# Operand places and dummy products in the three-part matrix products, and the last attention head's statistics turned by copies within SBUF

## The chip, the cores and the metric

The kernel runs on one core of a Trainium2 chip. The metric is the device time of one execution in microseconds (us). Three executions of the kernel before took 1504.59, 1506.12 and 1506.7 us; their median is 1506.12 us.

## What is computed

Two transformer layers on 512 tokens of width 1024, in fp32. Layer 0 mixes tokens with a gated linear recurrence, layer 1 with dilated attention in three groups of 8 heads; each is followed by a gated feed-forward network. Cut to what the change touches:

```python
def dilated_attention_mixer(u, cos, sin, w_in, w_out):
    proj = (u @ w_in).reshape(B, S, N_GROUPS, 3, ATT_HEADS, ATT_HEAD_DIM)   # 3 groups: (128,1) (512,4) (2048,16)
    for gi, (window, dilation) in enumerate(DILATED_GROUPS):
        q = apply_partial_rope(proj[:, :, gi, 0], cos, sin) * scale
        k = apply_partial_rope(proj[:, :, gi, 1], cos, sin)
        o_g, lse_g = dilated_group_attention(q, k, proj[:, :, gi, 2], window, dilation)
    wts = jax.nn.softmax(jnp.stack(lses, axis=0), axis=0)
    o = jnp.einsum('gbsh,gbshd->bshd', wts, jnp.stack(outs, axis=0))
    return o.reshape(B, S, D_MODEL) @ w_out

def swiglu_ffn(u, w_in, w_out):                     # D_FF = 2816 = 22 x 128
    gate, up = jnp.split(u @ w_in, 2, axis=-1)
    return (jax.nn.silu(gate) * up) @ w_out
```

## The kernel before, in words

**Three products for one.** Each operand is split into a high part (ACT, a cast to fp32r) and a low part (DVE, the difference). One product of 128x128 blocks becomes three fp32r matmuls: high by high, high by low, low by high (`three`, L576 to L579, and the loops at L964 and L1982). Each matmul has a stationary operand (128 columns, loaded by LDWEIGHTS) and a moving operand that streams past it.

**Seven for eight.** Most of the feed-forward input products (`seven_products`, L882), the queries and keys of groups 1 and 2 (`sevens`) and the values of groups 1 and 2 (`value_unit`) go by a scheme of seven half-size block products. They are *narrow*: the moving operand has 256 columns. One of the seven is a *unit*: 4 blocks of 128 rows, each by three matmuls, so 12 matmuls in a row into one PSUM place (a value product is two units, for two blocks of 128 tokens). The other products have a moving operand of 512 columns.

**The feed-forward stretches.** `seven_products` works through 16 functions (128 columns of gate and up) in layer 0 and 18 in layer 1. Per function `run` (L960) issues seven units: `first` with `B11`, `both` with `T3`, and so on. For function 0 `B11` is the first 256 tokens of `uh`, `ul` where they lie; then `shift()` (L893) copies them 144 columns further, and the functions after it take the copy.

**The attention as a plan.** Units, casts, softmax steps and DMAs of layer 1's attention are recorded as tasks with a cost and a due time (`Plan`); `Plan.run` tries 72 rules on a model of the engines and issues the best order, and each engine then runs its queue strictly in that order. `ticks` gives each head's steps their place: scores of group 0, of 1, of 2 (`scores_of`), the merge of the softmax statistics over groups (`merged`), transposes of the probabilities (`flipped`, PR for groups 1 and 2 by residue, PN for group 0), sums with the values (`sums_r`, `sums_n`). The 8 heads' output is multiplied by the output weights (`out_prods`, three matmuls of 512 columns, called a *group* below). The last head's late steps lie among the groups of the first columns of that product: after the products of each kt the table at L2446 says how many ticks to take.

**The turn of the statistics.** Group 0 has maximum and sum per token in natural order, groups 1 and 2 in residue order (token = 4 l + r). Both orders are needed in both places, so `scores_of` writes them to memory and reads them back in the other order: four DMAs on POOL's queue, L2261 (write of group 0's), L2281 (read back, "oR"), L2287 (write of the others'), L2289 (read back, "oN"). `merged` waits for both reads.

**Places.** By the addresses in the built program, the two operands of a narrow matmul start, modulo 256 bytes, here (all others of a kind alike, since blocks and tiles are multiples of 256 bytes apart):

| narrow matmuls | count | moving | stationary | stationary less moving |
|---|---|---|---|---|
| feed-forward, all but the next row (L964) | 2472 | 128 | 192 | 64 |
| feed-forward, `first` with the shifted `B11` (L964) | 384 | 192 | 192 | 0 |
| the first functions of a feed-forward and the like (L577 to L579, L825, L828) | 384 | 128 | 192 | 64 |
| queries and keys (L1982) | 1344 | 128 | 192 | 64 |
| values (L1982): the weights move, the tokens stand | 672 | 0 | 128 | 128 |

`R0` and `V0` (L37) are the columns by which the split tiles are set off: 16 fp32 (64 bytes) where weights are stationary, 32 (128 bytes) where value weights move.

Of the kernel before, what the change touches and what calls it, by code (L numbers as in the profile page):

```python
# [11 lines left out]
F32 = mybir.dt.float32  # L12
# [5 lines left out]
P = 128  # L18
# [3 lines left out]
NT = S // P  # L22
DFF = 2816
NF = DFF // P
NH = 8
# [11 lines left out]
R0, V0 = 16, 32  # L37
# [103 lines left out]
class Plan:  # L141
# [5 lines left out]
    def __init__(self):  # L147
        self.tasks, self.names, self.seq = [], {}, {}
# [144 lines left out]
def block_kernel(tc, x, c, positions, ada_w, ada_b, norm_g, hgrn_w_in, lower, hgrn_norm_g, hgrn_w_out,  # L293
                 attn_w_in, attn_w_out, ffn_w_in, ffn_w_out, inv_freq, out):
    nc = tc.nc
# [6 lines left out]
    with ExitStack() as ctx:  # L302
# [579 lines left out]
        def seven_products(fs, mid, seeded, spare, th, tl):  # L882
# [8 lines left out]
            B11 = [u_of(0, 0), [(uh[:, k, 144:400], ul[:, k, 144:400]) for k in range(4)]]  # L891

            def shift():  # L893

                for a, b in ((112, 256), (0, 112)):
                    for copy, t in ((act.copy, uh), (dve.tensor_copy, ul)):
                        copy(t[:, 0:4, a + 144:b + 144], t[:, 0:4, a:b].bitcast(F32))
# [77 lines left out]
            with tc.manual_schedule(engines=ORDERED):  # L975
# [10 lines left out]
                for i in range(len(fs)):  # L986
# [3 lines left out]
                    run(s.first, R, 0, B11[i > 0], True)  # L990
# [13 lines left out]
                    if i == 0:  # L1004
                        shift()
# [970 lines left out]
        def products(cost, dst, key, terms, begin, reads):  # L1976


            def go():
                todo = [p for t in terms() for p in t]  # L1980
                for i, (x, y) in enumerate(todo):
                    pe.matmul(dst(), x, y, start=begin and i == 0, stop=i == len(todo) - 1, skip_group_check=True)  # L1982
            of_units.append(len(plan.tasks))
            PE(cost, go, reads, [key])

# [119 lines left out]
        def plain(g, hd):  # L2105
# [16 lines left out]
            def both():  # L2122
# [4 lines left out]
                def one(i, t):  # L2127
                    b = mm_of()
                    for part in range(4):
# [4 lines left out]
                        products(6 * 0.2275, lambda: b.t, b(), terms, part == 0, [p("h", i), p("l", i)])  # L2134
# [15 lines left out]
        def value_unit(i, hf):  # L2150
# [46 lines left out]
            def run(tag, tile, o, us):  # L2197
                b, p = mm_of(tag), ps[tile]
                for n in range(2):
# [4 lines left out]
                    products(12 * 0.1165, lambda n=n: b.t[:, n * 256:(n + 1) * 256], b(), terms, n == 0, [p("h", o), p("l", o)])  # L2204
# [28 lines left out]

        def scores_of(hd, g):
# [3 lines left out]
            if g == 0:  # L2238
# [42 lines left out]
            POOL(0.6, lambda: pool.dma_start(so.t[:, 1, 0], scr[hd, 0].rearrange("(l r) s -> l r s", r=4)), [("scr", hd, 0)], [so("oR")], late=4.5)  # L2281
            DVE(0.12, lambda: dve.tensor_tensor(so.t[:, 0, 0, :, 0], mR.t[:, 0], mR.t[:, 1], op=OP.max), [mR(i, r) for i in (1, 2) for r in range(NT)], [so("R")])
            DVE(0.12, lambda: dve.tensor_scalar(nR.t, so.t[:, 0, 0, :, 0], -1.0, None, op0=OP.mult), [so("R")], [nR()])
            for r in range(NT):
                ACT(0.52, lambda r=r: act.activation(PR[:, r], PR[:, r], AF.Exp, bias=nR.t[:, r:r + 1], accum_out=so.t[:, 0, 0, r, 1:2]),
                    [nR(), so("R")], [("PR", 0, 1, r), ("PR", 0, 2, r), so("R", r)])
            POOL(0.6, lambda: pool.dma_start(scr[hd, 1].rearrange("(l r) s -> l r s", r=4), so.t[:, 0, 0]), [so("R")] + [so("R", r) for r in range(NT)],  # L2287
# [3 lines left out]
        def merged(hd):  # L2291
# [4 lines left out]
            reads = [so("R"), so("oR"), so("oN")] + [so(n, t) for n in "RN" for t in range(NT)]  # L2296
# [142 lines left out]
        for kt in range(KT):  # L2439
# [6 lines left out]
            for _ in range({0: 4, 1: 1, 2: 1, 3: 1, 5: 1, 6: 1}.get(kt, 0)):  # L2446
                ticks.tick()
# [53 lines left out]
```

## Time and profile before

| | us |
|---|---|
| median of 3 runs | 1506.12 |
| the profiled execution's own time | 1504.35 |
| its span, first to last instruction | 1502.6 |
| PE busy (matmul) | 1476.8 |
| DVE busy | 1095.8 |
| ACT busy | 797.2 |

The span is 1.75 us shorter than the execution; times of single instructions count from the span's start. PE is the engine of the matmuls (its weight loads are PEld), DVE, ACT and POOL are the vector, scalar and GpSimd engines, SP issues most DMAs. A matmul's duration in the profile (0.28 us for 256 columns) is its way through the array and overlaps its neighbours; what a stream costs is the distance from one start to the next, called the *pitch* here.

### The profile page before, as it was taken

How to read it: one execution, taken by the hardware profiler on the slowest of the kernel's cores; microseconds unless marked ns; L12 is line 12 of the kernel's file. 1: busy time of each engine (PE TensorE's matmuls, PEld its weight loads, DVE VectorE, ACT ScalarE, POOL GpSimd, SP SyncE). 2: the span in 40 equal slices, each digit the busy share in tenths (PEclk: the TensorE clock that was granted, in tenths of full speed). 3: DMA queues.
4: the chain of work that ended last, by engine and by line, in shares of the span. 5: the costliest groups of instructions: out<-in, count | busy, mean ns of one | idle time of the engine just before them, and what ended most of it. 6: DMA issues, size and time to landing. Idle time of an engine off the chain costs nothing. (4 is left out here: it accounts for less than half of the span.)

```text
span 1502.6 us, 25061 instructions
## 1 busy us (share of the span) xinstructions
PE 1476.8 (98%) x9823; PEld 1323.5 (88%) x9823; DVE 1095.8 (73%) x1800; ACT 797.2 (53%) x1474; POOL 191.3 (13%) x172
## 2 busy tenths in 40 slices
PE   8999999999999999999999999999989999999998
PEld 6777788888999988788999999999978899999886
DVE  4587678487688885777798877888666978887533
ACT  4433343373455542267647878477875555555231
POOL 1011011031111100131001010001012211110100
PEclk9999999999999999999999999999999999999999
DMA  9654555124233346634344442345243333333531
GB/s 308 183 170 140 183 169 169 57 79 146 85 113 113 113 161 211 220 117 143 113 120 144 109 136 73 118 131 147 89 134 119 104 94 113 113 113 141 197 111 56
DMA packets 210151, 201.09 MB, mean 134 GB/s; under 512 B 8248, under 2 KB 167920, under 8 KB 209776
## 3 DMA queue, kind: packets, MB, share of 16 engines
q1 hardware_dynamic: 207056, 192.71, 41.3%
q10 hardware_dynamic: 1952, 6.65, 1.2%
q8 instruction: 77, 1.26, 0.4%
q0 software_dynamic: 1024, 0.13, 0.2%
q14 instruction: 42, 0.34, 0.1%
HBM read 192.31 MB, written 5.31 MB: 132 GB/s over the span
## 5 line engine op out<-in xcount | busy, mean ns | idle before, releaser
L90 ACT CAST hi<-raw 128x2048 fp32r<-128x2048 f32 x43 | 82.1, 1909 | 144.3 <-DMA raw<-in_ffn_w_out_dram 74.9
L91 DVE TENSOR_TENSOR lo<-raw,hi 128x2048 fp32r<-128x2048 f32 x43 | 103.7, 2413 | 65.7 <-ACT hi L90 65.6
L577 PE MATMUL ps_mm<-uh,hi 128*128 128x512 f32 (+1 forms) x400 | 145.6, 364 | 0.0
L578 PE MATMUL ps_mm<-ul,hi 128*128 128x512 f32 (+1 forms) x400 | 144.5, 361 | 1.1 <-DVE ul L677 1.1
L579 PE MATMUL ps_mm<-uh,lo 128*128 128x512 f32 (+1 forms) x400 | 143.9, 360 | 0.0
L1982 PE MATMUL ps_mm<-apart,hiq 128*128 128x256 f32 (+1 forms) x608 | 142.0, 326 | 0.1
L1982 PEld LDWEIGHTS ps_mm<-apart,hiq 128*128 128x128 f32 x608 | 100.0, 189 | 8.4 <-ACT xs L2096 0.3
L1982 PE MATMUL ps_mm<-apart,loq 128*128 128x256 f32 (+1 forms) x304 | 97.4, 321 | 0.4 <-DVE loq L2118 0.4
L964 PE MATMUL ps_mm<-tl,hiq 128*128 128x256 f32 x340 | 94.0, 276 | 0.0
L964 PE MATMUL ps_mm<-th,hiq 128*128 128x256 f32 x340 | 94.0, 276 | 0.0
L964 PE MATMUL ps_mm<-th,loq 128*128 128x256 f32 x340 | 94.0, 276 | 0.0
L955 DVE TENSOR_TENSOR loq<-raw,hiq 128x1024 fp32r<-128x1024 f32 x68 | 80.3, 1221 | 18.6 <-ACT hiq L951 18.6
L577 PEld LDWEIGHTS ps_mm<-uh,hi 128*128 128x128 f32 x400 | 75.2, 188 | 18.2 <-issue 6.7
L578 PEld LDWEIGHTS ps_mm<-ul,hi 128*128 128x128 f32 x400 | 75.4, 189 | 12.3 <-DVE ul L677 1.5
L579 PEld LDWEIGHTS ps_mm<-uh,lo 128*128 128x128 f32 x400 | 75.1, 188 | 12.4 <-issue 1.1
L578 PE MATMUL ps_mm<-lo,oh 128*128 128x512 f32 x208 | 81.5, 392 | 2.4 <-DVE lo L91 2.4
L935 POOL TENSOR_TENSOR raw<-raw 128x512 f32<-128x512 f32 x34 | 44.8, 1318 | 303.1 <-DVE spare L931 138.5
L577 PE MATMUL ps_mm<-hi,oh 128*128 128x512 f32 x208 | 81.5, 392 | 0.0
L951 ACT CAST hiq<-raw 128x1024 fp32r<-128x1024 f32 x68 | 68.0, 1047 | 18.7 <-DVE raw L939 17.1
L1982 PE MATMUL ps_mm<-uh,hiq 128*128 128x256 f32 x256 | 71.9, 281 | 0.0
L1982 PE MATMUL ps_mm<-uh,loq 128*128 128x256 f32 x256 | 71.3, 279 | 0.0
L1982 PE MATMUL ps_mm<-ul,hiq 128*128 128x256 f32 x256 | 71.3, 278 | 0.0
(479 smaller groups left out, 4632.8 us busy)
## 6 DMA issues: line engine op xcount, KB each, us to landing
raw<-in_ada_w_dram SPq DMA_DIRECT2D x40, 1024.0 KB, 5.1
raw<-in_ffn_w_in_dram SPq DMA_DIRECT2D x136, 256.0 KB, 4.1
raw<-in_ffn_w_out_dram SPq DMA_DIRECT2D x22, 1024.0 KB, 5.1
raw<-in_attn_w_in_dram SPq DMA_DIRECT2D x64, 256.0 KB, 4.6
raw<-in_hgrn_w_in_dram SPq DMA_DIRECT2D x12, 1024.0 KB, 5.3
raw<-in_attn_w_in_dram SPq DMA_DIRECT2D x12, 1024.0 KB, 5.2
raw<-in_ffn_w_in_dram SPq DMA_DIRECT2D x10, 1024.0 KB, 6.5
raw<-in_attn_w_in_dram SPq DMA_DIRECT2D x16, 512.0 KB, 4.6
```

The source lines that it names most:

```text
L90: self.nc.scalar.copy(hi, t)
L91: self.nc.vector.tensor_sub(lo, t, hi.bitcast(F32))
L577: pe.matmul(ps, ah, bh, start=start, stop=False, skip_group_check=part)
L578: pe.matmul(ps, ah, bl, start=False, stop=False, skip_group_check=part)
L579: pe.matmul(ps, al, bh, start=False, stop=stop, skip_group_check=part)
L935: pool.tensor_add(r[:, 2], r[:, 2], r[:, 0])
L951: act.copy(hi, src)
L955: dve.tensor_sub(lo, src, hi.bitcast(F32))
L964: pe.matmul(ps, w[x][:, a], us[kt][y], start=begin and kt + m == 0, stop=kt == 3 and m == 2, skip_group_check=True)
L1982: pe.matmul(dst(), x, y, start=begin and i == 0, stop=i == len(todo) - 1, skip_group_check=True)
```

## The change

- `V0` is 48 columns: value weights move from 64 bytes modulo 256, the tokens stand at 128 as before, so the difference is 64, as with the other narrow products.
- `shift()` and the copy are gone; `first` takes `B11` where it lies for every function. Once per feed-forward, ahead of the second unit of function 0, three *dummy* matmuls are issued: the high weights (192) by `uh` from column 16 on (192), so with a difference of 0. Their result is overwritten by the unit that follows.
- In the attention `Plan.run` looks for stretches of narrow units and puts three such dummies (128 by 128 modulo 256) ahead of the first value unit that still has 12 units of its stretch to come. Two places come out: before the first unit of the first value stretch, and before the third unit of the second.
- The last head's statistics are turned by DMAs within SBUF, one per quarter: two on SP's queue and two on POOL's for oR, as many for oN, in place of the four POOL DMAs through memory.
- One tick is taken earlier: five after kt 0 rather than four, none after kt 6.

```diff
-R0, V0 = 16, 32
+R0, V0 = 16, 48
...
+        narrow = []
+        for t in [t for t in done if t["eng"] == "PE"] + [{}]:
+            if t.get("narrow"):
+                narrow.append(t)
+                continue
+            first = next((k for k, u in enumerate(narrow) if u["aside"]), len(narrow))
+            if len(narrow) - first >= 12:
+                self.asides.add(narrow[first]["id"])
+            narrow = []
...
-            B11 = [u_of(0, 0), [(uh[:, k, 144:400], ul[:, k, 144:400]) for k in range(4)]]
...
+            B11 = u_of(0, 0)
...
-                    run(s.first, R, 0, B11[i > 0], True)
+                    run(s.first, R, 0, B11, True)
+                    if i == 0:
+                        for _ in range(3):
+                            pe.matmul(s.both, R[0][:, 0:P], uh[:, 0, 16:272], start=True, stop=True, skip_group_check=True)
...
-                    if i == 0:
-                        shift()
...
+                for _ in range(3 if me in plan.asides else 0):
+                    pe.matmul(dst(), todo[0][0], aside(), start=True, stop=True, skip_group_check=True)
...
-                    products(12 * 0.1165, lambda n=n: b.t[:, n * 256:(n + 1) * 256], b(), terms, n == 0, [p("h", o), p("l", o)])
+                    products(12 * 0.1165, lambda n=n: b.t[:, n * 256:(n + 1) * 256], b(), terms, n == 0, [p("h", o), p("l", o)],
+                             lambda: p.t[0][:, o * 1024 + 16:o * 1024 + 272])
...
+        def turn_stats(t, pair, reads, key):
+            eng, queue_of, cost = (("SP", nc.sync, 0.55), ("POOL", pool, 0.65))[t % 2]
+            plan.add(eng, cost, lambda e: queue_of.dma_start(*pair()), reads, [key], late=2.8)
...
+                if straight(hd):
+                    for t in range(NT):
+                        turn_stats(t, lambda t=t: (quarter(so.t[t * 32:t * 32 + 32, 1, 0]), so.t[:, 0, 1, t]), [so("N", t)], so("oR", t))
+                    return
...
+            if straight(hd):
+                for t in range(NT):
+                    turn_stats(t, lambda t=t: (so.t[:, 1, 1, t], quarter(so.t[t * 32:t * 32 + 32, 0, 0])), [so("R")] + [so("R", r) for r in range(NT)],
+                               so("oN", t))
+                return
...
-            for _ in range({0: 4, 1: 1, 2: 1, 3: 1, 5: 1, 6: 1}.get(kt, 0)):
+            for _ in range({0: 5, 1: 1, 2: 1, 3: 1, 5: 1}.get(kt, 0)):
```

Where the instructions stand. PE in layer 0's feed-forward, at the border of the first and second unit of function 0; `spare` is that function's weight tile, `th`, `tl` token sums. Before:

```order
L964 MATMUL ps_a_3368<-ul,spare_3081 128x256
L964 MATMUL ps_a_3368<-uh,spare_3082 128x256
L964 MATMUL ps_a_3370<-th_3084,hiq_3374 128x256
L964 MATMUL ps_a_3370<-tl_3085,hiq_3374 128x256
L964 MATMUL ps_a_3370<-th_3084,loq_3375 128x256
```

Now:

```order
L967 MATMUL ps_a_3368<-ul,spare_3081 128x256
L967 MATMUL ps_a_3368<-uh,spare_3082 128x256
L996 MATMUL ps_a_3370<-uh,spare_3081 128x256 x3
L967 MATMUL ps_a_3370<-th_3084,hiq_3374 128x256
L967 MATMUL ps_a_3370<-tl_3085,hiq_3374 128x256
```

Three matmuls have come in, and nothing else has moved there; later functions have none.

PE around the last head's scores of group 2 (`qk,qk`), the transposes of PN of head 6 (`ident,h`), the output product's groups (`hiq`, `loq` by `oh`, `oT`) and head 6's `sums_n` (`h,V`). Before:

```order
L2273 MATMUL ps_a_10941<-qk_10598,qk_10597 128x128 x4
L2321 MATMUL ps_a_10925<-ident,h 128x128 x4
L577 MATMUL ps_mm_10833<-hiq_10714,oh_10872 128x512
L578 MATMUL ps_mm_10833<-loq_10715,oh_10872 128x512
L579 MATMUL ps_mm_10833<-hiq_10714,oT_10953 128x512
L577 MATMUL ps_mm_10851<-hiq_10714,oh_10872 128x512
L578 MATMUL ps_mm_10851<-loq_10715,oh_10872 128x512
L579 MATMUL ps_mm_10851<-hiq_10714,oT_10953 128x512
L2355 MATMUL ps_b_10667<-h,V_6096 128x128 x2
```

Now:

```order
L588 MATMUL ps_mm_10921<-hiq_10719,oT_10906 128x512
L2347 MATMUL ps_a_10948<-ident,h 128x128 x4
L2292 MATMUL ps_a_10949<-qk_10603,qk_10602 128x128 x4
L2381 MATMUL ps_b_10672<-h,V_6095 128x128 x2
L2383 MATMUL ps_b_10672<-h,V_6095 128x128
```

Two groups no longer stand between the transposes and `sums_n`; they follow later, behind the last head's own first transposes and sums. As many groups as before, 16, stand between `sums_n` of head 6 and the last head's transposes. Some 30 rows ahead of this place the two transposes of head 6's PR (eight matmuls) have moved from behind to before the last narrow unit of the attention (12 matmuls), and the last head's scores of group 1 from before to behind `sums_r` of head 6.

SP's queue at that time (weight and condition loads into `raw`). Before:

```order
L70 DMA raw_10883<-in_attn_w_out_dram 128x4x512
L70 DMA raw_10955<-in_ada_w_dram 128x4x512
L70 DMA raw_11033<-in_attn_w_out_dram 128x4x512
L70 DMA raw_11056<-in_attn_w_out_dram 128x4x512
L70 DMA raw_11144<-in_ffn_w_in_dram 128x8x256
```

Now:

```order
L70 DMA raw_10876<-in_attn_w_out_dram 128x4x512
L2247 DMA so_10374<-so_10374 32x4x2
L70 DMA raw_10963<-in_ada_w_dram 128x4x512
L2247 DMA so_10374<-so_10374 32x4x2
L2247 DMA so_10374<-so_10374 128x1x2 x2
L70 DMA raw_11047<-in_attn_w_out_dram 128x4x512
```

SP's four copies stand among the loads: one of oR's behind a load of 1024 KB, both of oN's ahead of the next two weight loads. POOL's queue has its four copies where the four DMAs of the last head were, with nothing else between.

More of the change, by code (lines that the diff above doesn't have):

```diff
@@ L2133, in terms @@
                                 yield triple(p.t[0][:, w], p.t[1][:, w], apart[0][:, kt], apart[1][:, kt])
-                        products(6 * 0.2275, lambda: b.t, b(), terms, part == 0, [p("h", i), p("l", i)])
+                        products(6 * 0.2275, lambda: b.t, b(), terms, part == 0, [p("h", i), p("l", i)], narrow=False)
                     scale = SCALE if i == 0 else 1.0
@@ L2280, in scores_of @@
                 return
-            POOL(0.6, lambda: pool.dma_start(so.t[:, 1, 0], scr[hd, 0].rearrange("(l r) s -> l r s", r=4)), [("scr", hd, 0)], [so("oR")], late=4.5)
+            if not straight(hd):
+                POOL(0.6, lambda: pool.dma_start(so.t[:, 1, 0], scr[hd, 0].rearrange("(l r) s -> l r s", r=4)), [("scr", hd, 0)], [so("oR")], late=4.5)
             DVE(0.12, lambda: dve.tensor_tensor(so.t[:, 0, 0, :, 0], mR.t[:, 0], mR.t[:, 1], op=OP.max), [mR(i, r) for i in (1, 2) for r in range(NT)], [so("R")])
@@ L2295, in merged @@
             so = st_["so"]
[L2296 removed]
+            turned_in = [so(n, t) for n in ("oR", "oN") for t in range(NT)] if straight(hd) else [so("oR"), so("oN")]
+            reads = [so("R")] + turned_in + [so(n, t) for n in "RN" for t in range(NT)]
             M, e, z = slot("wM", 2, [P, 2, NT], ap), slot("wE", 2, [P, 2, 2, NT], ap), slot("wZ", 2, [P, 2, 2, NT], ap)
```

14 lines of the change are left out of this document (7 added, 7 removed).

## The prediction

> **What bounds the kernel now.** First the page's header and the busy times.
>
> ```profile
> span 1502.6 us, 25061 instructions
> ...
> PE 1476.8 (98%) x9823; PEld 1323.5 (88%) x9823; DVE 1095.8 (73%) x1800; ACT 797.2 (53%) x1474; POOL 191.3 (13%) x172
> ```
>
> PE is busy for 98%, so time goes only where PE's stream gets shorter: through fewer products, a shorter pitch, or a wait less. Next the waits of PE, longest first; these two are the ones that the change touches.
>
> ```profile
> PE ps_a L2321 <- ACT h L2306: 2.7, 1, 2.7
> ...
> PE ps_a L2273 <- ACT h L2329: 2.2, 3, 1.3
> ```
>
> The first is the last head's transposes waiting for its merged probabilities. Then PE's timeline, for the pitch. These are the first matmuls of functions 0, 1 and 2 of layer 0's feed-forward, of the second and third unit of function 2, and of function 3; the first column is the start.
>
> ```profile
> 384.95 0.28 PE L964 MATMUL ps_a<-uh,spare 128*128 128x256 f32 x1
> ...
> 394.84 0.28 PE L964 MATMUL ps_b<-uh,hiq 128*128 128x256 f32 x1
> ...
> 404.45 0.28 PE L964 MATMUL ps_a<-uh,spare 128*128 128x256 f32 x1
> ...
> 405.88 0.29 PE L964 MATMUL ps_a<-th,hiq 128*128 128x256 f32 x1
> ...
> 407.25 0.28 PE L964 MATMUL ps_mm<-th,hiq 128*128 128x256 f32 x1
> ...
> 414.05 0.28 PE L964 MATMUL ps_b<-uh,hiq 128*128 128x256 f32 x1
> ```
>
> Function 0 takes 394.84 - 384.95 = 9.89 us for 84 matmuls, 117.7 ns each. Function 2 takes 9.60: its first unit (the shifted copy, operands 0 apart) 1.43 or 119 ns each, its second 1.37 or 114, and the other 60 matmuls 6.80 or 113.3. So the same shape at the same places (64 apart) runs at a long pitch, 117.7, or a short one, 113.3, and which of them is a state that lasts: it turned short behind the unit at 0 apart and held for the rest of the function.
>
> **Feed-forward.** With 113.3 throughout a function takes 84 x 113.3 = 9.52 us, so each of 32 functions (15 in layer 0, 17 in layer 1) saves 0.08 us: -2.56. Function 0 of each layer pays the first unit as now (1.41), three dummies at 119 (0.36), then 1.37 and 6.80: 9.94 against 9.89, +0.05 twice. Sum -2.46. Layer 1's stretch is as long as this pattern says, 9.89 + 9.61 + 16 x 9.60 = 173.1:
>
> ```profile
> 1203.42:1376.52 173.10, 172.99 (x1511) 173.02 (x1511) 1.00 0.37 110
> ```
>
> This rests on two things that no row shows: that three matmuls at 0 apart turn the state as twelve did, and that it then holds across the borders of functions. The bounds are -2.56 and the third rival's price. The copies of `shift` were on ACT and DVE, which wait for PE there; I take nothing for them.
>
> **Values.** The starts of a value unit and of the first unit after the stretch, for both stretches (the unit at 736.42 is the third of 28, that at 940.97 likewise):
>
> ```profile
> 736.42 0.28 PE L1982 MATMUL ps_a<-hiq,uh 128*128 128x256 f32 x1
> ...
> 773.85 0.40 PE L1982 MATMUL ps_mm<-apart,hiq 128*128 128x256 f32 x2
> ...
> 940.97 0.28 PE L1982 MATMUL ps_a<-hiq,uh 128*128 128x256 f32 x1
> ...
> 978.00 0.40 PE L1982 MATMUL ps_mm<-apart,hiq 128*128 128x512 f32 x1
> ```
>
> 26 units are 312 matmuls: 37.43 / 312 = 120.0 ns and 37.03 / 312 = 118.7, at 128 apart. Moved to 64 apart they are placed as the other narrow products, with both operands 64 bytes on; I take 113.3. That is 336 x 6.7 + 336 x 5.4 = 4.06 us less, and two lots of dummies, 0.72, more: -3.3. The ends: -4.1, and +0.7 if the new places do nothing. The state may outlive the stretch. The unit after the first stretch, and the six behind it, run long now although eight small score products (L2273) lie between; the second pair of rows is four units apart:
>
> ```profile
> 775.27 1.06 PE L2273 MATMUL ps_a<-qk,qk 128*128 128x128 f32 x8
> ...
> 777.58 0.28 PE L1982 MATMUL ps_mm<-uh,hiq 128*128 128x256 f32 x1
> ...
> 783.23 0.28 PE L1982 MATMUL ps_mm<-apart,hiq 128*128 128x256 f32 x1
> ```
>
> 5.65 / 48 = 117.7. If they start short, 84 x 4.4 ns = 0.37 us goes; the other end is 0. What bounds this stretch next is DVE, 35.95 us of 40.40:
>
> ```profile
> 733.40:773.80 40.40, 40.40 (x338) 40.37 (x337) 35.95 (x51) 18.99 (x27) 1.65 (x2) 1.00 0.34 108
> ```
>
> At 113.3 the stretch is 2.2 us shorter, 38.2, still above DVE's work; up to 1 us of waits stays in the range.
>
> A rule of the Trainium skill speaks against both terms: "TensorE: Matmul & The Clock Gate", Part 2, says that PE has two SBUF read ports, one for the streaming operand and one for LDWEIGHTS, and that loading the next weights takes no read bandwidth from the running matmul; its formula gives one gap for 256 columns, an estimated 109 ns, at any place. By it these terms would be nothing but the dummies' cost. The trace disagrees: 113.3, 117.7 and 120.0 ns for one shape.
>
> **The last head.** The chain: ACT's last exponentials, POOL's DMAs but the first, SP's weight loads, DVE's first merge step, then PE with its last group ahead of the transposes, the transposes, the groups behind them and `sums_r`; last the windows' row of that stretch (PE, PEld, DVE, ACT, POOL busy, then the granted clock).
>
> ```profile
> 1104.74 0.21 ACT L2285 ACTIVATION_READ_ACCUMULATOR h<-h,nR 128x1 f32 x1
> ...
> 1105.88 0.55 POOL L2281 DMA_DIRECT2D so<-scr  x1 [5.62 <-DMA scr<-so]
> 1106.50 0.56 POOL L2287 DMA_DIRECT2D scr<-so  x1
> 1110.09 0.76 POOL L2289 DMA_DIRECT2D so<-scr  x1 [3.03 <-DMA scr<-so]
> ...
> 1108.01 3.21 SPq L70 DMA_DIRECT2D raw<-in_attn_w_out_dram  x2
> ...
> 1115.42 0.17 DVE L2298 TENSOR_TENSOR wM<-so 128x8 f32<-128x8 f32 x1 [4.59 <-DMA so<-scr]
> ...
> 1114.44 0.39 PE L578 MATMUL ps_mm<-loq,oh 128*128 128x512 f32 x1
> 1114.67 0.39 PE L579 MATMUL ps_mm<-hiq,oT 128*128 128x512 f32 x1
> 1117.77 2.30 PE L2321 MATMUL ps_a<-ident,h 128*128 128x128 f32 x8 [2.72 <-ACT h L2306]
> 1119.72 0.78 PE L577 MATMUL ps_mm<-hiq,oh 128*128 128x512 f32 x1
> ...
> 1122.43 0.50 PE L2342 MATMUL ps_b<-h,V 128*128 128x128 f32 x2
> ...
> 1114.85:1122.45 7.60, 4.67 (x16) 3.32 (x16) 2.96 (x17) 5.45 (x13) 0.00 (x0) 0.79 0.10 37
> ```
>
> The hole: 1117.77 - 1114.67 less one 512-column pitch (0.23) is 2.87 us. Behind it the transposes and six products take 1122.43 - 1117.77 = 4.66; at full pace they take some 2.25 (transposes 0.76 from the first start to the last, 1.04 less one's 0.28 by the row of eight further below, six products 1.38, 0.1 between). That is 2.41 more, from ACT's pace in scaling and a clock that was granted at 0.79 on the mean. Together 5.28 us hang on the statistics being late.
>
> "TensorE: Matmul & The Clock Gate" of the Trainium skill, Part 1, has the clock halve after an idle window of about 3.4 us; by it a hole of 2.87 need not cost the clock, and the term would be nearer 3. The row, 0.79, has it lowered here, and the forecast goes by the row.
>
> Now two copies go out on each queue once the exponentials end (1104.95): two issues of about 0.6 each, 1106.2, then the landing. The nearest rows, a copy within SBUF by SP and the read back by POOL, from issue to landing:
>
> ```profile
> qk<-shared SPq DMA_DIRECT2D x56, 32.0 KB, 3.3
> ...
> so<-scr POOLq DMA_DIRECT2D x16, 4.0 KB, 3.4
> ```
>
> 1109.6; the merge needs 1117.77 - 1115.42 = 2.35, so 1112.0. PE gets there two groups earlier than now (6 x 0.23 = 1.4), at 1113.5: 1.5 us to spare, the whole 5.28 goes. At the other end the landing takes as long as this very read back did, 1115.42 - 1110.09 = 5.3: 1113.9, a wait of 0.4. What is queued behind: SP's next weight loads stand behind oN's copies, but the first of them is issued at 1108.01 now, when the copies are out. One of oR's copies stands behind a 1024 KB load; oR is due only with oN. POOL has only its reduction behind.
>
> The order also moves. Now the transposes of head 6's PR are followed by a wait:
>
> ```profile
> 1091.48 1.04 PE L2321 MATMUL ps_a<-ident,h 128*128 128x128 f32 x8
> ...
> 1093.81 1.16 PE L2273 MATMUL ps_a<-qk,qk 128*128 128x128 f32 x8 [1.29 <-ACT h L2329]
> ```
>
> With a narrow unit (1.4 us) behind the transposes it is covered: -1.3. But the two groups that covered ACT's copy ahead of head 6's `sums_n` are gone, and of their 1.4 us only the eight score products (0.9) remain; ACT has a cast and that copy to do meanwhile. I take +1.0 there, so -0.3 in all, with ends -1.3 and +0.9.
>
> **The sum.** -2.46 - 3.3 - 0.37 - 5.28 - 0.3 = -11.7 us, from the profiled execution's 1504.35 to 1492.6. The median of the runs is 1.77 above that execution, so 1494.4 beside it. Own range 1491 to 1497.5.
>
> **Rivals.**
>
> *The value products don't turn short* (0.14). For it: no narrow product with the moving operand at 64 is in the trace. Against it: difference and shape are those of products that do. At 117.7 they gain 1.1 less 0.72, at 120.0 they lose 0.7; without the 0.37 the sum is -8.4 to -7.3, median 1497.7 to 1498.8. By the two ports of the Trainium skill ("TensorE: Matmul & The Clock Gate", Part 2) it would come out at the latter end.
>
> *The statistics stay late* (0.08): the copies queue behind loads on shared engines, or are slow for their 8-byte pieces, and PE waits about as long as now. Then -2.46 - 3.3 - 0.37, 1500.0. It decides at 1.5 us over the landing I took.
>
> *Three dummies don't turn the state*, the slower side (0.11). Its place is function 0 of both feed-forwards, its point whether three matmuls at 0 apart do what twelve did. Then all 34 functions run at 9.89: 32 x 0.29 = +9.3, dummies +0.7; values at 117.7 gain 0.4, the last head 5.6: +4.0, 1510.1. For it: L2273's eight small products leave the state long (above). Against: eight small score products at another place did turn it. The starts of five units ahead of L2248 and five behind it:
>
> ```profile
> 798.54 0.28 PE L1982 MATMUL ps_mm<-uh,hiq 128*128 128x256 f32 x1
> ...
> 805.61 0.28 PE L1982 MATMUL ps_mm<-apart,hiq 128*128 128x256 f32 x1
> ...
> 809.93 0.28 PE L1982 MATMUL ps_mm<-uh,hiq 128*128 128x256 f32 x1
> ...
> 816.73 0.39 PE L1982 MATMUL ps_mm<-apart,hiq 128*128 128x256 f32 x2
> ```
>
> 7.07 / 60 = 117.8 ahead, 6.80 / 60 = 113.3 behind: a short disturbance can turn it. If one layer alone fails, the result lies near 1500.
>
> **How the numbers follow.** Forecast 0.67, 1494.4; rivals 0.14, 0.08, 0.11. From 1490.5 to 1501.5 the range holds the first three cases and leaves out the last, and little else. A measurement of this kernel can tell some 0.2%, 3.0 us, from no change. Forecast and the first two rivals lie beyond that, the third at +4 mostly so: faster 0.86, same 0.06, slower 0.08.
>
> **What would show it.** Right: functions after the first at 9.52 us in both layers with no unit at 119; value units at 1.36 us; no wait of over 0.5 us on the last head's transposes, and the clock at 1.0 there. Wrong: functions at 9.89 (dummies), value units at 1.41 or 1.44 (places), a DMA as releaser of the merge with PE idle (copies), or a new wait of PE on ACT's copies of more than 1.3 us about 1100.

## The result, and the profile after

The changed kernel takes 1493.97 us (median of 4 runs, 1492.70 to 1495.90), the kernel before 1505.36 beside it (4 runs, 1503.25 to 1506.70): a ratio of 0.9933, 95% interval 0.9920 to 0.9947. The profiled execution took 1492.70 us against 1504.35, 11.65 less; the forecast was 11.7 less. The total came out almost as predicted, its parts less so.

The busy times of the page after:

```profile
PE 1467.8 (98%) x9835; PEld 1315.0 (88%) x9835; DVE 1090.9 (73%) x1796; ACT 793.6 (53%) x1470; POOL 191.2 (13%) x172
```

PE still fills 98%: 12 matmuls more in 9 us less. PE's waits after, the ones that concern the change (total, times, longest):

```profile
PE ps_a L2292 <- ACT h L2355: 1.1, 1, 1.1
...
PE ps_b L2381 <- ACT h L2355: 0.4, 1, 0.4
```

The 2.7 us at the last head's transposes (now L2347) are gone from the list. The 0.4 is the new wait at head 6's `sums_n`; the 1.1 is the first head's, and nobody had forecast it.

PE's timeline after, for the feed-forwards: the dummies, the starts of functions 1 and 15 of layer 0, and of functions 1 and 17 of layer 1.

```profile
385.57 0.52 PE L996 MATMUL ps_a<-uh,spare 128*128 128x256 f32 x3
...
394.11 0.28 PE L967 MATMUL ps_b<-uh,hiq 128*128 128x256 f32 x1
...
527.39 0.28 PE L967 MATMUL ps_b<-uh,hiq 128*128 128x256 f32 x1
...
1202.77 0.28 PE L967 MATMUL ps_b<-uh,hiq 128*128 128x256 f32 x1
...
1355.09 0.28 PE L967 MATMUL ps_b<-uh,hiq 128*128 128x256 f32 x1
```

Fourteen functions in 133.28 us and sixteen in 152.32: 9.52 each, 113.3 ns a matmul, in both layers. The value stretches, from the third unit to the first unit behind the first stretch, and from the first unit behind the second lot of dummies to the end:

```profile
733.79 0.28 PE L1988 MATMUL ps_a<-hiq,uh 128*128 128x256 f32 x1
...
769.41 0.40 PE L1988 MATMUL ps_mm<-apart,hiq 128*128 128x256 f32 x2
...
938.64 0.29 PE L1988 MATMUL ps_a<-hiq,uh 128*128 128x256 f32 x1
...
974.02 0.63 PE L1988 MATMUL ps_mm<-apart,hiq 128*128 128x512 f32 x2
```

312 matmuls each: 114.2 and 113.4 ns, where 120.0 and 118.7 stood. (Two stalls of 0.11 us in the first make up the difference of 0.8 ns.) The last head: the end of ACT's exponentials, SP's and POOL's copies, DVE's last work ahead of the merge, the merge, ACT's scaling, the transposes; then the windows' row of the transposes and what follows (PE, PEld, DVE, ACT, POOL busy, granted clock).

```profile
1099.42 0.19 ACT L2305 ACTIVATION_READ_ACCUMULATOR h<-h,nR 128x1 f32 x1
...
1094.74 6.21 SPq L2247 DMA_DIRECT2D so<-so  x3
...
1099.91 1.11 POOL L2247 DMA_DIRECT2D so<-so  x2 [7.47 <-DVE shared L1945]
...
1102.33 1.22 DVE L2429 TENSOR_TENSOR loq<-raw,hiq 128x1024 fp32r<-128x1024 f32 x1
1103.46 0.16 DVE L2324 TENSOR_TENSOR wM<-so 128x8 f32<-128x8 f32 x1
...
1105.31 1.71 ACT L2332 ACTIVATE h<-h,wE 128x256 f32<-128x256 f32 x4 [1.23 <-DVE wE L2330]
...
1108.34 1.03 PE L2347 MATMUL ps_a<-ident,h 128*128 128x128 f32 x8
```

```profile
1108.30:1113.00 4.70, 4.70 (x37) 4.40 (x36) 1.69 (x2) 3.29 (x6) 2.67 (x1) 1.00 0.87 332
```

The copies are issued by 1101.0 and the last that the merge needs has landed by 1102.35 (the time is that of its semaphore in the trace); the merge starts at 1103.46, when DVE is done with the work ahead of it. The first of ACT's four scaled pieces is ready at 1105.83, the last at 1107.02, and PE comes at 1108.34: 2.5 us behind the first piece, 1.3 behind the last, with the clock at 1.00.

Stage by stage, from starts of matmuls in the two traces (us):

| stage | before | after | difference | forecast |
|---|---|---|---|---|
| up to layer 0's feed-forward | 383.76 | 382.96 | -0.80 | 0 |
| feed-forward, layer 0 | 153.91 | 152.76 | -1.15 | |
| feed-forward, layer 1 | 184.05 | 182.73 | -1.32 | -2.46 for both |
| from layer 0's feed-forward to the values | 194.50 | 193.61 | -0.89 | 0 |
| first value stretch | 40.50 | 38.90 | -1.60 | |
| second value stretch | 42.63 | 41.30 | -1.33 | -3.3 for both |
| heads between the stretches | 161.52 | 163.31 | +1.79 | -0.37 |
| the last heads, the output product | 167.79 | 161.16 | -6.63 | -5.58 |
| the rest | 166.16 | 166.17 | 0 | 0 |

The stages add up to 11.9 us less; the span is 11.6 less, since the tail behind the last matmul is 0.3 longer. The fourth row is no work of the change. The windows of the same stretch of layer 0's output product, first before, then after:

```profile
600.00:610.00 10.00, 8.15 (x31) 6.33 (x30) 9.12 (x17) 2.43 (x2) 3.23 (x1) 0.86 0.57 188
```

```profile
598.00:608.00 10.00, 8.02 (x36) 6.28 (x35) 9.08 (x18) 2.44 (x2) 3.23 (x1) 1.00 0.57 184
```

The same wait of 2.0 and 2.15 us stands in both, and the clock fell behind it only in the execution of before (0.86 over 10 us; by the trace's clock records half speed for 3.4 us, which makes some 1.7 us lost).

### The profile page after: what moved, and what is told of

The parts are those of the page before. It is cut to its first block, busy times and chain, and to the rows that moved or that the text cites. A ratio compares the mean times of both kernels' runs of the same rounds, so it can differ in the third digit from the quotient of the medians.

```text
span 1491.0 us, 25093 instructions
## 1 busy us (share of the span) xinstructions
PE 1467.8 (98%) x9835; PEld 1315.0 (88%) x9835; DVE 1090.9 (73%) x1796; ACT 793.6 (53%) x1470; POOL 191.2 (13%) x172
## 3 DMA queue, kind: packets, MB, share of 16 engines
q0 software_dynamic: 1024, 0.12, 0.2%
```

## The experiments

The theory: the pitch of narrow products is a state that lasts, equal places turn it short, and V0 = 48 gives the values places at which it can be short; the last head's gain comes from copies that land in time. The rival of most weight was that the dummies do nothing, or not everywhere. Ratios are to the kernel before on the same chip, whose medians lay between 1501.64 and 1503.08 there; the changed kernel's own ratio is 0.9933. Runs 2, 6, 7, 10, 11 and 12 are one execution each; they are read by their stages alone.

### 1. No dummies

```diff
-                        for _ in range(3):
+                        for _ in range(0):
...
-                for _ in range(3 if me in plan.asides else 0):
+                for _ in range(0 if me in plan.asides else 0):
```

> The changed kernel without its dummies at all four places (two feed-forwards, two value stretches); nothing else differs. Theory (the pitch is a state that lasts, and three matmuls with operands 0 apart turn it): all 34 functions of the feed-forwards run at 9.89 us instead of 9.52, 32 x 0.37 = +11.8 and the two first functions at 9.89 less their dummies; value units at 1.41 us instead of 1.36, 672 x 4.4 ns = +3.0; the dummies' 1.4 go; the 1.1 us of waits at 812 to 816 us go, because PE gets there later. Together about +12, near 1506 us. Rival A (the state turns by itself once the copies are gone, the dummies do nothing): functions at 9.52, 1492.6 us. Rival B (the dummies matter in the feed-forwards, the values need only the new places): +11.1, about 1505 us with value units at 1.36.

Measured: 1509.47 us, ratio 1.0039 (1.0024 to 1.0054), slower than the kernel before. The starts of functions 1 and 15 of layer 0, and 1 and 17 of layer 1:

```profile
395.55 0.28 PE L967 MATMUL ps_b<-uh,hiq 128*128 128x256 f32 x1
...
534.06 0.28 PE L967 MATMUL ps_b<-uh,hiq 128*128 128x256 f32 x1
...
1212.74 0.28 PE L967 MATMUL ps_b<-uh,hiq 128*128 128x256 f32 x1
...
1371.03 0.28 PE L967 MATMUL ps_b<-uh,hiq 128*128 128x256 f32 x1
```

138.51 / 14 and 158.29 / 16 are 9.89 us a function; the value units ran at 117.8 ns. Against the changed kernel the feed-forwards cost 5.53 and 6.30 us, the value stretches 0.87 and 1.00. The rest of the distance lies in stages that the change doesn't touch and that differ from execution to execution: the start and layer 0's output product took 3.9 us more here (the clock was at half for 3.4 us from 14 and from 151 us on, and not in the changed kernel's profiled execution), the heads between the value stretches 1.6 less. The theory holds, rivals A and B fall. This is also the price of the forecast's third rival: +11.8 us in the feed-forwards over the changed kernel, +9.4 over the kernel before.

### 2. Dummies 64 apart

```diff
-                            pe.matmul(s.both, R[0][:, 0:P], uh[:, 0, 16:272], start=True, stop=True, skip_group_check=True)
+                            pe.matmul(s.both, R[0][:, 0:P], uh[:, 0, 0:256], start=True, stop=True, skip_group_check=True)
...
-                             lambda: p.t[0][:, o * 1024 + 16:o * 1024 + 272])
+                             lambda: p.t[0][:, o * 1024:o * 1024 + 256])
```

> The changed kernel with the three dummies at each of the four places put 64 bytes apart (moving operand from column 0 of its block instead of 16), as the products around them; their number is the same. Theory (it is the equal place that turns the state): they turn nothing; functions at 9.89 us in both layers, value units at 1.41, about 1507 us. Rival (any three products more, or the short break that they make in the order, turn it): functions at 9.52, value units at 1.36, 1494 us.

Measured: 1507.97 us. Functions 1 and 15 of layer 0:

```profile
395.41 0.28 PE L967 MATMUL ps_b<-uh,hiq 128*128 128x256 f32 x1
...
533.91 0.28 PE L967 MATMUL ps_b<-uh,hiq 128*128 128x256 f32 x1
```

9.89 us again, so in layer 1, and 117.8 ns in both value stretches. Three products more do nothing by themselves; it is their place.

### 3. Values 128 apart again

```diff
-R0, V0 = 16, 48
+R0, V0 = 16, 32
...
-                for _ in range(3 if me in plan.asides else 0):
+                for _ in range(0 if me in plan.asides else 0):
```

> The changed kernel with V0 at 32 again and without the two lots of dummies ahead of the values. Theory (the value stretches gained some 3.3 us, and some 1.3 of these were given back in waits at 755 to 816 us, where PE comes to ACT's and DVE's work sooner): value units at 1.44 and 1.42 us, +4.06 and -0.72, and the waits of 1.39 us behind the last product before the transposes and of 0.47 at 812 us gone: about +2.0, near 1496 us. Rival (those waits have nothing to do with the values' pace): they stay, +3.3, near 1497.3 us.

Measured: 1496.07 us, ratio 0.9951 (0.9936 to 0.9965). The stretches took 1.61 and 1.33 us more than in the changed kernel, 2.94 together, as between the two kernels. The heads between them took 1.50 less, which looks like the theory's give-back, and the time is the theory's 1496; run 6 shows that this is luck. What differs is a DMA. POOL's read back of the first head's statistics waits for their write to memory (in brackets), in the changed kernel:

```profile
806.48 0.76 POOL L2314 DMA_DIRECT2D so<-scr  x1 [2.58 <-DMA scr<-so]
```

and in run 6, whose values are as fast:

```profile
808.09 0.76 POOL L2314 DMA_DIRECT2D so<-scr  x1 [1.42 <-DMA scr<-so]
```

There the heads between the stretches took 161.89 us, near the 161.52 of before. The wait for the write was 1.41 or 1.42 us in the kernel before and in runs 1, 3, 6 and 10, where these heads took 161.5 to 161.9 us; it was 2.42 to 3.17 in the changed kernel and in runs 2 (whose values are slow), 4, 11 and 12, where they took 162.8 to 164.8. Run 5 lies between (2.14 and 162.2), and run 7 (1.41 and 163.6) has other waits. So the 1.79 us go with a late write, which delays the first head's merge, ACT's scaling and PE behind it, and not with the values' pace. This is read from the traces: no run changes the write alone, and what delays it is not settled.

### 4. Statistics through memory

```diff
-        straight = lambda hd: hd == NH - 1
+        straight = lambda hd: False
```

> The changed kernel with the last head's statistics through memory again, the ticks as changed. Theory (it is the copies that bring the statistics in time): from the last exponential's end (1099.6 us) the chain takes the 10.5 us of before to the merge, 1110.1 instead of 1103.5; the scaled probabilities come about 1112.5, PE stands ready at 1108.3: a hole of about 4 us and a lowered clock behind it (below 0.85 over the 7 us that follow) for 2.4 more, about +6.5, near 1500.5 us. Rival (the earlier tick alone had brought enough): a hole under 1.5 us, the clock at 1.0, under 1495.5 us.

Measured: 1501.72 us, ratio 0.9991 (0.9982 to 1.0000), about 8.7 us over the changed kernel. PE's longest wait, and the windows' row behind it:

```profile
PE ps_a L2347 <- ACT h L2332: 3.7, 1, 3.7
```

```profile
1112.90:1120.50 7.60, 7.60 (x32) 6.37 (x33) 5.92 (x9) 5.99 (x12) 3.23 (x1) 0.58 0.43 138
```

The tick alone makes it worse: PE comes sooner, the statistics don't. The stage with the last head is 8.6 us longer than in the changed kernel, more than the 6.5 expected. The clock was at half for 6.8 us (0.58 in the row), where the kernel before had it so for 3.4; and the plan's order moved too, so that PE waits 1.6 us for ACT ahead of the last head's scores, which the changed kernel doesn't. The theory holds.

### 5. Ticks as before

```diff
-            for _ in range({0: 5, 1: 1, 2: 1, 3: 1, 5: 1}.get(kt, 0)):
+            for _ in range({0: 4, 1: 1, 2: 1, 3: 1, 5: 1, 6: 1}.get(kt, 0)):
```

> The changed kernel with the table of ticks of before (four after the first columns, one after the seventh); the copies stay. Theory (the copies alone bring the statistics in time; the earlier tick only swaps one wait for another): no wait over 0.5 us at the last head's transposes; the wait of 1.29 us ahead of the last head's second lot of scores is back, the new ones of 0.54 and 0.37 us there go: +0.4 to +0.9, about 1494.6 us. Rival (the fillers that the ticks move are what covers the chain): a wait of over 1.5 us at the transposes, 1496 us or more.

Measured: 1496.76 us, ratio 0.9960 (0.9944 to 0.9976). The end of the exponentials, SP's queue (a 1024 KB weight load, then one of the copies), the merge, the transposes:

```profile
1104.09 0.19 ACT L2305 ACTIVATION_READ_ACCUMULATOR h<-h,nR 128x1 f32 x1
...
1105.05 0.55 SPq L70 DMA_DIRECT2D raw<-in_attn_w_out_dram  x1
1105.65 0.60 SPq L2247 DMA_DIRECT2D so<-so  x1
...
1110.85 0.17 DVE L2324 TENSOR_TENSOR wM<-so 128x8 f32<-128x8 f32 x1 [2.61 <-DMA so<-so]
...
1113.21 1.96 PE L2347 MATMUL ps_a<-ident,h 128*128 128x128 f32 x8 [0.56 <-ACT h L2332]
```

The theory falls: the copies alone don't suffice. The weight load stands ahead of one copy, which lands 4.8 us after its issue. It is not the queue alone: the copy that POOL issued at 1105.14, just behind the load but on another queue, took 3.5 us, and the two issued ahead of the load 1.7 and 1.8. The merge starts 6.6 us after the exponentials (3.9 in the changed kernel). PE waits 0.7, and the transposes start 0.40 us apart, at ACT's pace in scaling, three times. The stage of the last heads is 2.5 us longer than in the changed kernel, the wait of 0.9 us ahead of the scores included.

### 6. One dummy, or two

```diff
-                        for _ in range(3):
+                        for _ in range(1 if len(fs) == 16 else 2):
...
-                for _ in range(3 if me in plan.asides else 0):
+                for _ in range(1 + (me != min(plan.asides)) if me in plan.asides else 0):
```

> The changed kernel with one dummy instead of three ahead of layer 0's feed-forward and of the first value stretch, and two ahead of layer 1's and of the second. Theory (one matmul with equal places is enough to turn the state): functions at 9.52 us and value units at 1.36 everywhere, about 0.7 us less than with three, 1492 us. Rival A (two are needed): layer 0's functions at 9.89, +5.5, and the first stretch's units at 1.41, +1.5. Rival B (three are needed): both layers at 9.89 and all value units at 1.41, about +14.

Measured: 1493.62 us. The starts of functions 1 and 17 of layer 1, with two dummies:

```profile
1203.65 0.28 PE L967 MATMUL ps_b<-uh,hiq 128*128 128x256 f32 x1
...
1355.97 0.28 PE L967 MATMUL ps_b<-uh,hiq 128*128 128x256 f32 x1
```

9.52 us, in layer 0 too, and 113.3 and 113.4 ns in the value stretches. The four stages together took 0.98 us less than with three. The theory seemed to hold; runs 8 and 12 overturn it.

### 7 and 10. Places in a row

Run 7 has a row of blocks of 24 products in place of layer 0's three dummies; run 10 another (number of products, first column of the moving operand; the column decides the place).

```diff
-                        for _ in range(3):
-                            pe.matmul(s.both, R[0][:, 0:P], uh[:, 0, 16:272], start=True, stop=True, skip_group_check=True)
+                        for n, c, a in table if len(fs) == 16 else [(3, 16, 0)]:
+                            for _ in range(n):
+                                pe.matmul(s.both, R[0][:, a:a + P], uh[:, 0, c:c + 256], start=True, stop=True, skip_group_check=True)
```

> The changed kernel with a measuring row in place of the three dummies of layer 0's feed-forward: blocks of 24 narrow products that are overwritten, each foreign place followed by 24 at the usual one (64 apart): one, two, three products at 0 apart; 128 apart (twice); both operands moved by 64 (so 64 apart still); then 32, 96, 192 and 48 apart; three at 0 at the end. It adds some 465 products, about 54 us. Theory (the pitch is a state of 113.3 or 117.7 ns that equal places set to short and that 128 apart sets to long): usual blocks at 117.7 first, 113.3 behind each lot at 0 apart, 117.7 behind 128 apart; the blocks at 0 and at 128 apart at 118.4 to 120. Rival (only the place itself decides, with no memory): all usual blocks read the same. What 32, 48, 96 and 192 apart do, neither says; each block's pitch, and that of the usual block behind it, is what the run is for.

PE's timeline of run 7. Each row is 21 of a block's 24 products, from the fourth on; its length less 0.28, by 20, is the pitch. In order: usual; usual behind one at 0 apart; 128 apart; usual; usual behind three at 0 apart; both operands moved by 64; usual.

```profile
387.40 2.64 PE L999 MATMUL ps_a<-uh,spare 128*128 128x256 f32 x21
...
390.34 2.56 PE L999 MATMUL ps_a<-uh,spare 128*128 128x256 f32 x21
393.10 2.65 PE L999 MATMUL ps_a<-uh,spare 128*128 128x256 f32 x21
395.94 2.64 PE L999 MATMUL ps_a<-uh,spare 128*128 128x256 f32 x21
...
407.77 2.64 PE L999 MATMUL ps_a<-uh,spare 128*128 128x256 f32 x21
410.60 2.64 PE L999 MATMUL ps_a<-uh,spare 128*128 128x256 f32 x21
413.43 2.55 PE L999 MATMUL ps_a<-uh,spare 128*128 128x256 f32 x21
```

118, 114 (113.3 over the last twelve), 118.5, 118, 118, 118, 113.5. There is a memory, against the rival: the same places give both pitches. But three at 0 apart left it long, and behind a block with both operands moved by 64, with the distance unchanged, it was short. Behind the blocks at 32, 96, 192 and 16 apart (the last is the one that the expectation calls 48) it was short too, as it had been ahead of them.

> A second measuring row in place of the three dummies of layer 0's feed-forward, overwritten like the first: six times 24 products at 128 apart (which left the long pitch both times before), 12 at the usual 64 apart, then 1 to 6 products at 0 apart, then 24 at 64 apart; after that five times 24 at 128 apart and 36 at 48, 56, 40, 72 and 80 apart. It adds some 680 products, about 80 us. Theory A (equal places always turn the state; the one lot of three that did not in the first row was an exception of its own): 113.3 ns behind all six counts. Theory B (a product at another place is a kick, and what follows depends on where in the long pattern it comes): some counts leave 117.7. For the distances between 40 and 80: if 113.3 comes by itself from the long side, a place needs no dummies; by the first row (32 and 96 apart gave 118.1 and 117.2) I expect 117 or more at all of them.

Usual blocks of run 10 behind 2, 3 and 4 products at 0 apart:

```profile
400.75 2.54 PE L998 MATMUL ps_a<-uh,spare 128*128 128x256 f32 x21
...
408.10 2.64 PE L998 MATMUL ps_a<-uh,spare 128*128 128x256 f32 x21
...
415.64 2.64 PE L998 MATMUL ps_a<-uh,spare 128*128 128x256 f32 x21
```

113, 118 and 118; behind 1, 5 and 6 it was short. Ahead of 1, 4 and 5 it had been short already, and the four turned it back to long. The runs fit theory B: a product at another place is a kick, not a switch. Blocks of 24 at 128 apart show it best, for in the two rows they turned the pitch over each time before usual blocks: five that met the short pitch ran at 118.5 and left it long, three that met the long one ran at 120.0 and left it short. At 40, 48, 56, 72 and 80 apart the pitch is 119 to 121 ns; of all the places tried only 64 apart ever gave 113.3 in a steady run. (The two patterns at 128 apart, 118.5 and 120.0, are also those of the two value stretches of before, 118.7 and 120.0.)

### 8 and 9. More heads copied, one dummy

```diff
-        straight = lambda hd: hd == NH - 1
+        straight = lambda hd: hd in (0, NH - 1)
```

with one dummy at all four places; run 9 has `True` for all heads.

> The changed kernel with one dummy at each of the four places instead of three, and with the first head's statistics turned by copies within SBUF as the last head's are. Theory (the wait of 1.0 to 2.2 us that PE has near 813 us in some runs comes from the first head's write to memory, which took 1.4 us where nothing was in its way and 2.6 to 3.2 where it was): the first head's merge comes sooner and no wait of over 0.3 us stands there; one dummy saves 0.7 us; together 0.7 to 2 us less than the changed kernel, a ratio to the kernel before of about 0.992. Rival (the copies on SP's queue put the next weight loads off, so that PE waits for a cast elsewhere): the gain is eaten, a ratio of 0.9933 or more.

> As the kernel before this in the row, with all eight heads' statistics turned by copies. Theory (only the first and the last head's statistics are on PE's path; the others have time): the same time as with the first and the last head's, within 1 us, though the plan's order changes with the costs. Rival A (every head gains by it): under 0.990. Rival B (eight copies per head load SP's queue and the DMA engines and put off the weights): slower than the changed kernel by 1 us or more.

Measured: 1501.69 us, ratio 0.9993 (0.9982 to 1.0004), and 1501.19, 0.9990 (0.9981 to 0.9999). Run 8: SP's queue and the first head's merge, then functions 1 and 17 of layer 1.

```profile
806.47 2.33 SPq L68 DMA_DIRECT2D raw<-in_attn_w_in_dram  x2
808.85 1.31 SPq L2247 DMA_DIRECT2D so<-so  x2
...
813.75 0.17 DVE L2324 TENSOR_TENSOR wM<-so 128x8 f32<-128x8 f32 x1 [2.46 <-DMA so<-so]
...
1205.90 0.28 PE L967 MATMUL ps_b<-uh,hiq 128*128 128x256 f32 x1
...
1364.20 0.28 PE L967 MATMUL ps_b<-uh,hiq 128*128 128x256 f32 x1
```

Two things went wrong. One dummy left layer 1's functions at 158.30 / 16 = 9.89 us in both runs: 6.41 us, most of the loss, and the reason that the totals say nothing on the copies. And the first head's copies stand behind two weight loads on SP's queue, with the exponentials themselves later in the new plan, so that the merge came at 813.75 (810.78 in the changed kernel). The heads between the value stretches took 164.82 and 164.53 us against 163.31: the theory on the first head falls for this way of doing it. (In run 9 PE waited 1.8 us there, and the clock was at half for 3.4 us behind it.) In run 9 a stall of 0.6 us in the first value stretch, in its 21st unit, was followed by 117.8 in place of 113.3 for the eight units left: a wait can be a kick too. It need not be: in run 5 a stall as long, at the same matmul, left the pitch short, and so did one of 0.3 in run 9's second stretch.

### 11. Ticks as before, copies on POOL

```diff
-            eng, queue_of, cost = (("SP", nc.sync, 0.55), ("POOL", pool, 0.65))[t % 2]
+            eng, queue_of, cost = (("SP", nc.sync, 0.55), ("POOL", pool, 0.65))[t % 2 or key[2] == "oN"]
```

together with the edit of run 5.

> The changed kernel with the ticks of before, as in the fifth run, but with all four copies of the second turn on POOL's queue, so that none stands behind SP's weight load. Theory (in the fifth run one copy went out behind a weight load of 1024 KB and landed 5.2 us after its issue; that made PE's wait of 0.7 and the slow transposes): four issues end 2.2 us after the exponentials, land 2.4 later, the merge starts about 4.7 us after the last exponential's end instead of 6.6, and PE waits under 0.2 us for the scaled probabilities. Rival (the load on the shared engines makes every copy late, whatever its queue): the merge starts 6 us or more after the exponentials, the wait stays above 0.5.

Measured: 1495.27 us. DVE's work ahead of the merge, POOL's reduction, DVE's second merge step and PE's transposes:

```profile
1106.87 1.53 DVE L1945 SCALAR_TENSOR_TENSOR shared<-raw,cond,shared 128x512 f32<-128x512 f32 x2
...
1108.51 3.23 POOL L1948 PARTITION_ALL_REDUCE shared<-shared  x1 [3.11 <-DVE wM L2324]
...
1108.52 2.25 DVE L2325 TENSOR_TENSOR wE<-so,wM 128x16 f32<-128x16 f32 x1
...
1112.76 1.96 PE L2347 MATMUL ps_a<-ident,h 128*128 128x128 f32 x8
```

The wait at the transposes is gone, which the theory asked and the rival denied; the merge starts 5.4 us after the exponentials, between the two. The copies are not what it waits for: each landed 1.6 or 1.7 us after its issue, the last 3.6 us after the exponentials, sooner than the theory had it, and DVE was busy with other work until the merge. (The 5.2 us of the expectation run on to run 5's merge; the copy itself landed after 4.8.) Then a merge step of 0.17 us took 2.25 beside the start of POOL's reduction, the transposes run at ACT's pace again, and the wait ahead of the scores is 1.0. So the stage is still 1.8 us over the changed kernel's. By these traces the earlier tick earns its 1.8 to 2.5 us in three places: that wait, SP's order, and PE's arrival behind ACT's scaling.

### 12. Four dummies

```diff
-                        for _ in range(3):
+                        for _ in range(4):
...
-                for _ in range(3 if me in plan.asides else 0):
+                for _ in range(4 if me in plan.asides else 0):
```

> The changed kernel with four dummies at each of the four places instead of three. So far three turned the pitch short at all four places; one did so in layer 0's feed-forward and not in layer 1's; in the second measuring row one, two, five and six left it short, three and four long. Theory (a product at equal places is a kick to a phase, and the pitch that follows depends on where in the long pattern it comes, so that more dummies are no safer than fewer): at least one of the four stretches stays at 117.7 to 117.8 ns; a feed-forward that stays long costs 5.5 us in layer 0, 6.3 in layer 1, a value stretch about 1.5. Rival (three or more are enough within the kernel, and the rows failed for the products at 128 apart ahead of them): all four stretches at 113.3, 0.5 us over the changed kernel.

Measured: 1494.87 us. The first value stretch, third unit to the first unit behind it:

```profile
735.12 0.28 PE L1988 MATMUL ps_a<-hiq,uh 128*128 128x256 f32 x1
...
771.87 0.40 PE L1988 MATMUL ps_mm<-apart,hiq 128*128 128x256 f32 x2
```

36.75 / 312 = 117.8 ns: this stretch stayed long, the other three were short. The theory holds: more dummies are no safer. For a given place and count the outcome repeated from run to run: three in layer 0 short in the changed kernel and four runs more, one in layer 1 long in both runs that had it.

## Why the prediction was right, point by point

- **Feed-forward**, -2.46: measured -2.47, and runs 1 and 2 show the cause, products at another place than the usual one. The third rival (0.11) did not come about, but runs 8 and 12 show that it was a matter of the count: one dummy in layer 1 loses 6.4 us. The words "three matmuls at 0 apart turn the state as twelve did" held here; as a rule they fail (runs 7 and 10), so that three being a count that works at all four places is luck.
- **Values**, -3.3: measured -2.94. The pitch was right, 113.3; short of the forecast are two stalls of 0.11 and two units ahead of the second lot that stay at 118. The bound from DVE's work held. The Trainium skill's two independent read ports ("TensorE: Matmul & The Clock Gate", Part 2) would have left only the dummies' cost of 1.4 us here; run 1, where their absence costs 11.8, does not agree.
- **The seven units behind the stretch**, -0.37: measured 0, its other end. They ran at 117.8 as before. The unit directly behind the stretch, ahead of the eight score products, is already at 117.6, so the step from the values' places to the usual ones, both moved by 64, is itself a kick, as in run 7.
- **The last head and the order**, -5.28 and -0.3: measured -6.63 together, 6.3 of it around the last head. The hole (2.88) and the slow stretch behind it (2.41) were sized right; the order's part was mis-sized, since the 1.29 us wait went and the new one cost 0.5 rather than 1.0. That makes 6.05 of the 6.3; the rest is not traced. The spare time, which the forecast counts up to the first scaled piece, came out at 2.5 us, forecast 1.5. The 2.35 us from the merge's start to that piece held; the copies landed in 1.7 to 2.0 us rather than 3.4, and of that gain DVE, busy until 1103.46, took back 1.1. What the forecast did not see is that the tick also takes the copies past the weight load on SP's queue. "The first of them is issued at 1108.01 now, when the copies are out" holds only with the earlier tick (run 5).
- **Not forecast**: +1.79 in the heads between the value stretches (a late write), -0.89 (a clock that fell in the execution of before alone), -0.80 up to the first feed-forward. They nearly cancel, so that the total is right to 0.1 us by some luck; its terms miss by up to 1. What stands ahead of the first feed-forward took 383.0 to 386.3 us in the runs, though no edit touches it.

## What to carry to other kernels

Where one shape shows two pitches, look at the operands' addresses modulo a few hundred bytes and at what came just before, and price the state by the whole stretch behind it: three products of 0.36 us decide on 5.5 to 6.3 us. A trick that sets such a state must be measured at every place and after every change of the program, since its success at one count tells nothing of the next. And a short copy is only as fast as the loads around it allow: look at what stands ahead of it on its queue, and at what is issued beside it on the others, before its latency.

## What the runs showed of the hardware

- This kernel's narrow matmul, with its operands 64 bytes apart, has two steady pitches, 113.3 and 117.8 ns, and keeps the one it has for 1500 matmuls; at 0, 16, 32, 40, 48, 56, 72, 80, 96, 128 and 192 apart the steady runs showed 117 to 121 ns. Which one follows a product at another place depends on the count, and on the pitch that it meets, in a way that the runs don't explain; a stall of 0.6 us turned it once (run 9) and once not (run 5).
- Copies of 1 KB within SBUF landed in some 2 us (medians 1.9 on POOL, 2.0 on SP in the changed kernel), behind a weight load of 1024 KB on their own queue in 6.2 (changed kernel) and 4.8 (run 5), and beside such a load on another queue in 3.5 (run 5). The Trainium skill ("DMA: Bandwidth & Descriptors", on the anatomy of one DMA) has a fixed cost of about 2.0 us for a DMA issued by GpSimd; POOL's 1.9 agrees.
- Holes of PE of 2.9 and 3.7 us lowered the clock to half, for 3.4 and 6.8 us; one of 0.7 did not, nor one of 2.4 (run 1, at 613 us), and of two of 2.0 and 2.15 us at one place only the shorter did. A wait of 1.8 us (run 9, at 815 us) lowered it, and so did a wait of 1.5 to 1.7 near 151 us in seven of the 14 traces. The Trainium skill ("TensorE: Matmul & The Clock Gate", Part 1) has the clock fall after an idle window of some 3.4 us, in windows that run freely; that the outcome varies agrees with it, that 1.5 to 2.0 us can suffice does not.
